# A streaming-encoder block in split fp32: start addresses of weights and moving tiles, and seven other offsets in one product

## The chip, the core and the metric

The kernel runs on one NeuronCore of a Trainium2 chip. The metric is device time in microseconds of one execution, lower is better. One launch computes the whole block; weights and input lie in the chip's DRAM, and the working set is tiled into the core's on-chip memory, SBUF, which has 128 partitions. An address below is a byte offset within a partition.

## The reference, cut to what matters

One layer, 512 tokens, 1024 channels, all in float32:

```python
x = x + 0.5 * swiglu(rms_norm(x, ffn1_norm), ffn1_w1, ffn1_w3, ffn1_w2)      # D_FF = 2816
p = rms_norm(x, mix_norm) @ w_in
y_a = rwkv7_mixer(...) @ rwkv_proj       # delta rule, 8 heads x 64
y_b = fox_mixer(...) @ fox_proj          # forgetting attention, 8 heads x 64
x = x + (gate_a * y_a + gate_b * y_b) @ w_out
x = x + 0.5 * swiglu(rms_norm(x, ffn2_norm), ffn2_w1, ffn2_w3, ffn2_w2)
out = rms_norm(x, final_norm)

def swiglu(h, w1, w3, w2):
    return (silu(h @ w1) * (h @ w3)) @ w2
```

## The kernel before

Channels stand on the partitions, the 512 tokens along the free axis. The input is transposed into eight tiles xT of 128 x 512. A matmul takes a weight tile of 128 x 128 as its stationary operand and a tile of 128 x 512 as its moving operand, and accumulates into one bank of PSUM.

**Split products.** For the accuracy of float32 every operand is split in two float32r tiles, hi (a rounded copy) and lo (what is left). `mm3` (L124) then issues three matmuls for one product: hi by hi, hi weights by lo moving, lo weights by hi moving (L125 to L127). Nearly all of TensorE's time is in these three lines.

**Weights.** `load_raw` issues one DMA on the SyncE queue into one of 3 `raw` buffers. `split_w` (L111) makes `whi` with a cast on ScalarE (L117) and `wlo` with a subtract on VectorE (L118), each in one of 2 buffers. So a weight piece can be cast only when TensorE has finished the piece two before it, and loaded only when the piece three before it has been split.

**Stages, in the order of time.** The first FFN: for each of 22 column tiles the products `pa` and `pb` over 8 normalized tiles xh/xl, then on VectorE and ScalarE silu and product into hh and hl, 22 tiles each. Its last product `pd` (L340 to L346) runs over 8 output tiles m and, for each, over 22 k-tiles; the 22 weight tiles come in the pieces of `cuts` (L338): 8, 8 and 6 k-tiles. Then the mixer: projections of w_in (`pl`, `pk`, `pgt`, `pq`, `pv`), the RWKV recurrence and the attention with many short matmuls, the two output projections `ppj` (moving yh/yl, then ya) and w_out's `pw` (moving mh/ml). Then the second FFN with the same function `ffn`; its `pd` has seven output tiles of this kind. After each, VectorE adds the result to the residual tile xS, TensorE transposes that (`ot`), and VectorE writes it with the final gain into O. The eighth output tile has weights of its own (`ownh`, `ownl`) and runs in two halves of 256 tokens.

**What sets the order.** Tiles come from pools that allocate SBUF one after the other, on the left and the right side, so that a tile's address follows from the sizes of those before it. The instruction order of each engine is made by a scheduler in the program's build, from a timeline of its own; engines synchronize through semaphores.

Of the kernel before, what the change touches and what calls it, by code (L numbers as in the profile page):

```python
# [9 lines left out]
F32 = mybir.dt.float32  # L10
F32R = mybir.dt.float32r
BF16 = mybir.dt.bfloat16
AF = mybir.ActivationFunctionType
ALU = mybir.AluOpType
# [4 lines left out]
P = 128  # L19
T = 512  # L20
D = 1024
KD = D // P
# [3 lines left out]
NP = DA // P  # L26
C = 32
NC = T // C
NB = T // P
# [6 lines left out]
PAR_W0, PAR_A0, PAR_KK, PAR_KA, PAR_RK, PAR_LG, PAR_LB = 38, 42, 46, 50, 54, 58, 62  # L36
PAR_Q, PAR_K, PAR_F = 66, 67, 68
PAR_N = 69

COL_W = 3 * DA  # L40
COL_G = COL_W + 64
# [9 lines left out]
def kernel(  # L51
# [7 lines left out]
    dve, act, pool, pe = nc.vector, nc.scalar, nc.gpsimd, nc.tensor  # L59

    cp = ctx.enter_context(tc.tile_pool(name="cp", bufs=1))
    xp = ctx.enter_context(tc.tile_pool(name="xp", bufs=1))
    wp = ctx.enter_context(tc.tile_pool(name="wp", bufs=2))
    tp = ctx.enter_context(tc.tile_pool(name="tp", bufs=4))
# [5 lines left out]
    def bank(name, pool_=None):  # L70
        pool_ = pool_ or pm
        return pool_.tile([P, T], F32, tag="b", name=name)

    def tmp(name, shape=(P, T), dt=F32, tag="t", **kw):
        return tp.tile(list(shape), dt, tag=tag, name=name, **kw)
# [3 lines left out]
    make_identity(nc, ident)  # L79
    identb = cp.tile([P, P], BF16, name="identb")  # L80
    dve.tensor_copy(identb[:], ident[:])
    ones = cp.tile([P, P], F32, name="ones")
    dve.memset(ones[:], 1.0)
    onesr = cp.tile([P, P], F32R, name="onesr")
    dve.tensor_copy(onesr[:], ones[:])
    bones = tmp("bones", (P, P))
    dve.memset(bones[:], 0.0)
    dve.memset(bones[0:64, 0:64], 1.0)
# [15 lines left out]
    def load_raw(aps, kt, n):  # L104
        raw = wp.tile([P, kt, n], F32, tag="raw", name="raw", bufs=3)
        for c0, src in aps:
            nc.sync.dma_start(raw[:, :, c0:c0 + src.shape[1]],
                              src.rearrange("(k p) c -> p k c", p=P))
        return raw

    def split_w(raw, kt, n, eng=None, own=None):  # L111
        if own is None:
            hi = wp.tile([P, kt, n], F32R, tag="whi", name="whi", bufs=2)
            lo = wp.tile([P, kt, n], F32R, tag="wlo", name="wlo", bufs=2)
        else:
            hi, lo = [xp.tile([P, kt, n], F32R, tag=f"x{i}{own}", name=f"own{i}{own}") for i in "hl"]
        act.copy(hi[:], raw[:])  # L117
        (eng or dve).tensor_tensor(lo[:], raw[:], hi[:].bitcast(F32), op=ALU.subtract)  # L118
        return hi, lo

    def load_w(aps, kt, n, eng=None, own=None):
        return split_w(load_raw(aps, kt, n), kt, n, eng, own)

    def mm3(ps, whi, wlo, xhi, xlo, first, last):  # L124
        pe.matmul(ps, whi, xhi, start=first, stop=False)  # L125
# [78 lines left out]

    par = cp.tile([P, PAR_N], F32, name="par")

# [5 lines left out]
    nc.scalar.dma_start(g1[:], ffn1_norm[0].rearrange("(a b) -> a b", b=P))  # L212
    warm = bank("warm", pf)
    for _ in range(8):
        pe.matmul(warm[:, 0:P], ones[:], ones[:], start=True, stop=True)
    gtp = bank("gtp", pr)
    pe.transpose(gtp[:, 0:8], g1[:], ident[0:8, 0:8])
    dve.tensor_copy(par[:, 0:8], gtp[:, 0:8])
# [28 lines left out]
    tc.keep_in_program_order(pin)  # L247
    rows = rtp.tile([PAR_N, P], F32, name="rows")
    loraw = rtp.tile([P, DA], F32, name="loraw")
# [45 lines left out]
    def place_params():  # L295
        ptp = bank("ptp")
        pe.transpose(ptp[:, 0:PAR_N], rows[:], ident[0:PAR_N, 0:PAR_N])
        dve.tensor_copy(par[:, 8:PAR_N], ptp[:, 8:PAR_N])
        dve.tensor_scalar(par[:, PAR_Q:PAR_Q + 1], par[:, PAR_Q:PAR_Q + 1], 0.125, None, op0=ALU.mult)
# [8 lines left out]
    def ffn(nrm, w1, w3, w2, nxt, during=(), first=None, final=None):  # L308
        with tc.tile_pool(name="hp", bufs=1) as hp:
            hh, hl = [], []  # L310
            for j in range(KF):
                c0 = j * P
                if j == 0 and first:
                    pa, pb = [f[0] for f in first]
                else:
                    pa = bank("pa")
                    pb = bank("pb", pr)
                    for ps, w in ((pa, w1), (pb, w3)):
                        nrm.cols(ps[:], *load_w([(0, w[0][:, c0:c0 + P])], KD, P), P)
                if j == 0:  # L320
                    nrm.finish()
                if j in during:
                    with tc.issue_after(pin.ins):
                        during[j]()
                a = tmp("fa")
                dve.tensor_tensor(a[:], pa[:], nrm.rstd[:], op=ALU.mult)  # L326
                sa = tmp("fs")
                act.activation(sa[:], a[:], AF.Silu)
                b = tmp("fb")
                dve.tensor_tensor(b[:], pb[:], nrm.rstd[:], op=ALU.mult)  # L330
                h = tmp("fh")
                dve.tensor_tensor(h[:], b[:], sa[:], op=ALU.mult)
                hi = hp.tile([P, T], F32R, name=f"hh{j}")
                lo = hp.tile([P, T], F32R, name=f"hl{j}")
                split(hi[:], lo[:], h[:], "dve")
                hh.append(hi)
                hl.append(lo)
            cuts = ((0, 8), (8, 8), (16, 6))  # L338

            for m in range(KD - (final is not None)):  # L340
                ps = bank("pd")
                for k0, kn in cuts:
                    wh, wl = load_w([(0, w2[0][k0 * P:(k0 + kn) * P, m * P:(m + 1) * P])], kn, P)
                    for k in range(k0, k0 + kn):
                        mm3(ps[:], wh[:, k - k0, :], wl[:, k - k0, :], hh[k][:], hl[k][:], k == 0, k == KF - 1)
                dve.scalar_tensor_tensor(xT[m][:], ps[:], 0.5, xT[m][:], op0=ALU.mult, op1=ALU.add)  # L346
                nxt(m)
            if final is not None:
                m = KD - 1
                quarters = [(k0, min(4, KF - k0)) for k0 in range(0, KF, 4)]  # L350
                ws = [load_w([(0, w2[0][k0 * P:(k0 + kn) * P, m * P:(m + 1) * P])], kn, P, own=i)
                      for i, (k0, kn) in enumerate(quarters)]
                for h in range(2):
                    ps = bank("pd")
                    cols = slice(h * T // 2, (h + 1) * T // 2)
                    for (k0, kn), (wh, wl) in zip(quarters, ws):
                        for k in range(k0, k0 + kn):
                            mm3(ps[:, 0:T // 2], wh[:, k - k0, :], wl[:, k - k0, :], hh[k][:, cols], hl[k][:, cols],
                                k == 0, k == KF - 1)
                    dve.scalar_tensor_tensor(xT[m][:, cols], ps[:, 0:T // 2], 0.5, xT[m][:, cols],  # L360
                                             op0=ALU.mult, op1=ALU.add)
                    final(h)
# [16 lines left out]
    with ExitStack() as mx:  # L379
        rp = mx.enter_context(tc.tile_pool(name="rp", bufs=1))  # L380
# [13 lines left out]

        nka = rp.tile([P, NP], F32, name="nka")
        dve.tensor_scalar(nka[:], par[:, PAR_KA:PAR_KA + NP], -1.0, None, op0=ALU.mult)
        tiny = rp.tile([P, 2], F32, name="tiny")
        dve.memset(tiny[:, 0:1], 1e-24)
        dve.memset(tiny[:, 1:2], -1e-24)
        omu = rp.tile([P, PAR_W0 - PAR_MU], F32, name="omu")  # L400
        dve.tensor_scalar(omu[:], par[:, PAR_MU:PAR_W0], -1.0, 1.0, op0=ALU.mult, op1=ALU.add)

        def shifted(o, src, rows, mu):
            act.activation(o[0:rows, :], src[0:rows, :], AF.Copy, scale=omu[0:rows, mu - PAR_MU:mu - PAR_MU + 1])
# [49 lines left out]
        xctx.close()  # L454
        fctx = ExitStack()
        vtp = fctx.enter_context(tc.tile_pool(name="vtp", bufs=1, side="right"))
        pctx = ExitStack()
        t2 = pctx.enter_context(tc.tile_pool(name="t2", bufs=1, side="right"))
        cmask = t2.tile([P, T], F32, name="cmask")
        pool.memset(cmask[:], 1.0)  # L460
        pool.memset(cmask[:].rearrange("p (c t) -> p c t", t=C)[:, :, 0:1], 0.0)

        PC = rp.tile([P, NP, NC], F32, name="PC")
        Ld = dp.tile([P, C, C], F32, name="Ld")
        Td = dp.tile([P, C, C], F32, name="Td")
        V4 = rp.tile([P, NP, T], F32, name="V4", tag="V4")
# [142 lines left out]
        for t in range(C - 1):  # L609
            n, m = t + 1, C - 1 - t  # L610
# [7 lines left out]
        for i in range(2):  # L618
            for q in range(2):
                o = i * 64 + q * C  # L620
# [57 lines left out]
        vt = []  # L678
# [6 lines left out]
                    mm3(vps[b][:], mix.hi[kk][:, bs], mix.lo[kk][:, bs], wh[:, k, :], wl[:, k, :],  # L685
                        kk == 0, kk == KD - 1)
        for b in range(NB):
            o = vtp.tile([P, T], F32, name=f"vt{b}", tag=f"vt{b}")
            act.activation(o[:], vps[b][:], AF.Copy, scale=rc[:, b:b + 1])
            vt.append(o)  # L690
        plain_gate(NP)
# [10 lines left out]
        for q in range(2):  # L702
            pool.memset(Rs[0][half(q), :, q, :], 0.0)
            for i in range(4):
                o = (1 - q) * 64
# [21 lines left out]
        for c in range(NC):  # L727
# [3 lines left out]
            for p, q in heads():  # L731
                o = (p // 2) * 64 + q * C
# [41 lines left out]
        for q in range(2):  # L774
            o = (1 - q) * 64
            pool.memset(f32(klc[q][:]), 0.0)
            dve.tensor_copy(klc[q][o:o + 8, :], fz[FR, :])
        for q in range(2):
            o = (1 - q) * 64
# [8 lines left out]
        for p in range(NP):  # L788
# [5 lines left out]
            for q in range(2):  # L794
# [6 lines left out]
                dve.tensor_tensor(klc[q][h_, :], kp[h_, :], f32(kb[q][h_, :]), op=ALU.subtract)  # L801
                act.copy(qb[q][h_, :], qp[h_, :])
                dve.tensor_copy(qb[q][g_, :], sel[g_, h:h + 1].broadcast_to([64, T]))
            mx_ = [tp.tile([P, 2 * NB], F32, tag=f"mx{q}", name=f"mx{q}", bufs=2) for q in range(2)]
            for i, bl in enumerate(((0, 1), (2,), (3,))):
                at = {b: sum(c + 1 for c in bl[:j]) * P for j, b in enumerate(bl)}
                w = sum(b + 1 for b in bl) * P
                lps, trs = [], []
                for q in range(2):
                    lp = pf.tile([P, T], F32, tag="b", name="lp")  # L810
                    lps.append(lp)
                    for b in bl:
                        n, bs = (b + 1) * P, slice(b * P, (b + 1) * P)
# [4 lines left out]
                for q in range(2):  # L818
                    pt, mx = pts[:, q], mx_[q]
                    for b in bl:  # L820
                        n, mb = (b + 1) * P, mx[:, b:b + 1]
# [17 lines left out]
                for j, b in enumerate(bl):  # L839
                    for k in range(b + 1):  # L840
                        o = at[b] + k * P
# [61 lines left out]
        for p in range(NP):  # L903
            o = vtp.tile([P, T], F32R, name=f"yh{p}", tag=f"vt{p}")
# [39 lines left out]
        for m in range(KD):  # L944
            wh, wl = load_w([(0, w_out[0][:, m * P:(m + 1) * P])], KD, P)
# [78 lines left out]
```

## Time and profile before

| | |
|---|---|
| timed runs, median (lowest to highest) | 1213.7 us (1209.55 to 1213.95), 3 runs |
| span of the profiled execution | 1210.2 us (its time beyond the span is not listed) |
| TensorE busy | 1184.5 us of the span, 6334 matmuls |
| VectorE, ScalarE, GpSimd busy | 665.2, 458.1, 100.5 us |
| mean granted TensorE clock | 0.992 |
| DMA | 122.54 MB, mean 101 GB/s |

How to read it: the span is from the first to the last instruction of one execution. A matmul's record reaches from its start to its modelled end and overlaps the next one's, so the time that a matmul costs is read from one start to the next, not from its duration. A row of the timeline gives start and duration in us, engine, line, operation, the tile written and those read; a row of the windows view gives length, then each engine's busy time with its count, the granted clock, the DMA share and GB/s. A row of the view of one tile gives minimum, median and maximum duration in ns, and the first and last start in us.

### The profile page before, as it was taken

What the parts mean: (1) busy time and instruction counts of PE and PEld (TensorE: products, weight loads), DVE (VectorE), ACT (ScalarE), POOL (GpSimd) and SP (SyncE); (2) the same over time, 40 slices, a digit from 0 to 9 for tenths busy, and PEclk for the clock granted to TensorE, in tenths of its full rate; (3) what the DMA queues carried; (4) which work ended last, traced back from release to release, by engine and by line L of the source; (5) the groups of instructions that cost most, each with busy time, mean ns of one, the idle gap of its engine ahead of it and who ended that gap; (6) DMA issues with size and microseconds to landing.
All of it is one profiled execution on the core that took longest, in us unless ns stands there. A gap on an engine that the chain in (4) does not pass through costs nothing.

```text
span 1210.2 us, 15874 instructions
## 1 busy us (share of the span) xinstructions
PE 1184.5 (98%) x6334; PEld 955.1 (79%) x6334; DVE 665.2 (55%) x993; ACT 458.1 (38%) x739; POOL 100.5 (8%) x144
## 2 busy tenths in 40 slices
PE   8999999999999999999999999999999999999997
PEld 6788888888887788887667777678888888888887
DVE  7454555443443688776766666865554445443232
ACT  5222222222222854445867655523322222222221
POOL 4100000001111111321000011111000000000110
PEclk9999999999999999999999999999999999999999
DMA  6233233333334234345113235532333333323331
GB/s 186 73 95 105 87 105 88 104 95 108 107 111 106 76 104 124 109 135 131 36 36 102 63 97 163 178 106 87 103 102 92 100 104 88 104 80 96 96 96 70
DMA packets 208152, 122.54 MB, mean 101 GB/s; under 512 B 9902, under 2 KB 200430, under 8 KB 208078
## 3 DMA queue, kind: packets, MB, share of 16 engines
q1 hardware_dynamic: 202078, 108.67, 31.1%
q0 software_dynamic: 3760, 12.06, 3.2%
q8 instruction: 50, 0.82, 0.3%
q10 hardware_dynamic: 2240, 0.79, 0.3%
q14 instruction: 24, 0.20, 0.1%
HBM read 110.82 MB, written 10.68 MB: 100 GB/s over the span
## 4 chain that ended last, share of the span: by engine, by line
PE 93%; DVE 3%; ACT 1%; issue 0%; DMA 0%; DVEq 0%; POOL 0%; POOLq 0%
PE pd L127 7%; PE pd L125 7%; PE pd L126 7%; PE pa L125 7%; PE pa L126 7%; PE pa L127 6%; PE pb L127 6%; PE pb L126 6%; PE pb L125 6%; PE pgt L125 3%; PE pgt L127 2%; PE pgt L126 2%; PE pk L125 2%; PE pk L127 2%; PE pk L126 2%; PE pw L127 1%
## 5 line engine op out<-in xcount | busy, mean ns | idle before, releaser
L117 ACT CAST whi<-raw 128x1024 fp32r<-128x1024 f32 (+3 forms) x199 | 198.2, 998 | 631.2 <-PE pa L126 180.7
L118 DVE TENSOR_TENSOR wlo<-raw,whi 128x1024 fp32r<-128x1024 f32 (+2 forms) x198 | 229.5, 1159 | 142.3 <-ACT whi L117 142.2
L125 PE MATMUL pa<-xh,whi 128*128 128x512 f32 x344 | 134.7, 392 | 2.6 <-DVE fa L326 2.6
L127 PE MATMUL pb<-xh,wlo 128*128 128x512 f32 x344 | 134.5, 391 | 0.9 <-DVE wlo L118 0.9
L126 PE MATMUL pa<-xl,whi 128*128 128x512 f32 x344 | 134.6, 391 | 0.0
L125 PE MATMUL pb<-xh,whi 128*128 128x512 f32 x344 | 134.5, 391 | 0.0
L126 PE MATMUL pb<-xl,whi 128*128 128x512 f32 x344 | 134.5, 391 | 0.0
L127 PE MATMUL pa<-xh,wlo 128*128 128x512 f32 x344 | 134.4, 391 | 0.0
L127 PE MATMUL pd<-hh,wlo 128*128 128x512 f32 x330 | 130.8, 396 | 0.0
L125 PE MATMUL pd<-hh,whi 128*128 128x512 f32 x330 | 130.3, 395 | 0.0
L126 PE MATMUL pd<-hl,whi 128*128 128x512 f32 x330 | 130.3, 395 | 0.0
L330 DVE TENSOR_TENSOR fb<-pb,rstd 128x512 f32<-128x512 f32 x43 | 29.7, 691 | 137.5 <-PE pb L127 137.5
L125 PEld LDWEIGHTS pa<-xh,whi 128*128 128x128 f32 x344 | 64.9, 189 | 16.7 <-DVE fa L326 3.1
L127 PEld LDWEIGHTS pb<-xh,wlo 128*128 128x128 f32 x344 | 65.0, 189 | 14.8 <-DVE wlo L118 1.3
L127 PEld LDWEIGHTS pa<-xh,wlo 128*128 128x128 f32 x344 | 65.0, 189 | 13.6
L126 PEld LDWEIGHTS pa<-xl,whi 128*128 128x128 f32 x344 | 65.0, 189 | 13.5
L126 PEld LDWEIGHTS pb<-xl,whi 128*128 128x128 f32 x344 | 65.0, 189 | 13.5
L125 PEld LDWEIGHTS pb<-xh,whi 128*128 128x128 f32 x344 | 64.9, 189 | 13.5
L126 PEld LDWEIGHTS pd<-hl,whi 128*128 128x128 f32 x330 | 62.0, 188 | 14.9
L125 PEld LDWEIGHTS pd<-hh,whi 128*128 128x128 f32 x330 | 62.0, 188 | 14.6
L127 PEld LDWEIGHTS pd<-hh,wlo 128*128 128x128 f32 x330 | 62.0, 188 | 14.6
L326 DVE TENSOR_TENSOR fa<-pa,rstd 128x512 f32<-128x512 f32 x43 | 29.7, 692 | 73.6 <-PE pa L127 73.6
(395 smaller groups left out, 1968.0 us busy)
## 6 DMA issues: line engine op xcount, KB each, us to landing
raw<-in_ffn_w_dram SPq DMA_DIRECT2D x118, 512.0 KB
raw<-in_w_in_dram SPq DMA_DIRECT2D x40, 512.0 KB
raw<-in_ffn_w_dram SPq DMA_DIRECT2D x15, 384.0 KB
raw<-in_w_out_dram SPq DMA_DIRECT2D x8, 512.0 KB
gsave<-gs SPq DMA_DIRECT2D x9, 256.0 KB
xin<-in_x_dram SPq DMA_DIRECT2D x4, 512.0 KB
xsave<-xT POOLq DMA_DIRECT2D x8, 256.0 KB, 2.3
G<-gsave POOLq DMA_DIRECT2D x8, 256.0 KB, 3.8
```

Source lines behind the costliest of these rows:

```text
L117: act.copy(hi[:], raw[:])
L118: (eng or dve).tensor_tensor(lo[:], raw[:], hi[:].bitcast(F32), op=ALU.subtract)
L125: pe.matmul(ps, whi, xhi, start=first, stop=False)
L126: pe.matmul(ps, whi, xlo, start=False, stop=False)
L127: return pe.matmul(ps, wlo, xhi, start=False, stop=last)
L326: dve.tensor_tensor(a[:], pa[:], nrm.rstd[:], op=ALU.mult)
L330: dve.tensor_tensor(b[:], pb[:], nrm.rstd[:], op=ALU.mult)
```

## The change

No product, no dtype and no buffer count changes. Two things do.

**Start addresses.** Three small constants are moved or padded: `ones` becomes a view of `onesr` with its first copy in a temporary buffer, `tiny` and `mx_` are padded to 32 columns, `PC` is allocated earlier, the `vt` tiles are allocated when their pool is opened, with 48 columns behind them. The tiles after them shift. In the program as built, byte addresses modulo 512 are:

| operands of a product | before | after |
|---|---|---|
| all weights (whi, wlo, ownh, ownl) of full 128-column tiles | 288 | 288 (but see below) |
| xh, xl (moving in `pa`, `pb`, `pk`, `pgt`, `pq`) | 288 | 288 |
| hh, hl (moving in `pd`) | 416 | 288 |
| ya, mh, ml (moving in `ppj`, `pw`) | 320 | 288 |
| yh, yl (moving in the first `ppj`) | 480 | 288 |
| kb, klc, qa (attention) | 480 | 288 |

A full weight tile is 512 bytes wide and a moving tile 2048, so a whole row of k-tiles keeps its place modulo 512. Only weights that are cut narrower (`pl`, 72 and 96 columns) wander.

**The second FFN's last product.** There, for the output tiles m = 0 to 6, `split_w` puts hi and lo at `PLACES[m]` columns into a buffer of full size. The weights thus start 4 * PLACES[m] bytes further than the moving tile, modulo 512: 256, 128, 64, 32, 16, 448 and 192. To leave room for it, `cuts` has there four pieces of 6, 6, 6 and 4 k-tiles in place of 8, 8 and 6. The first FFN keeps its three pieces and its place 0.

```diff
+PAD = 32
+PLACES = (64, 32, 16, 8, 4, 112, 48)
...
-    ones = cp.tile([P, P], F32, name="ones")
-    dve.memset(ones[:], 1.0)
+    ones_ = tmp("ones", (P, P))
+    dve.memset(ones_[:], 1.0)
     onesr = cp.tile([P, P], F32R, name="onesr")
-    dve.tensor_copy(onesr[:], ones[:])
+    dve.tensor_copy(onesr[:], ones_[:])
+    ones = onesr[:].bitcast(F32)
...
-    def split_w(raw, kt, n, eng=None, own=None):
-        if own is None:
+    def split_w(raw, kt, n, eng=None, own=None, place=0):
+        if place:
+            hi, lo = [wp.tile([P, KD * P], F32R, tag=f"w{i}", name=f"w{i}", bufs=2) for i in ("hi", "lo")]
+            hi, lo = [t[:, place:place + kt * n].rearrange("p (k c) -> p k c", c=n) for t in (hi, lo)]
+        elif own is None:
...
-            cuts = ((0, 8), (8, 8), (16, 6))
+            cuts = ((0, 8), (8, 8), (16, 6)) if final is None else ((0, 6), (6, 6), (12, 6), (18, 4))
...
-                    wh, wl = load_w([(0, w2[0][k0 * P:(k0 + kn) * P, m * P:(m + 1) * P])], kn, P)
+                    wh, wl = load_w([(0, w2[0][k0 * P:(k0 + kn) * P, m * P:(m + 1) * P])], kn, P,
+                                    place=0 if final is None else PLACES[m])
...
-        tiny = rp.tile([P, 2], F32, name="tiny")
+        tiny = rp.tile([P, PAD], F32, name="tiny")
...
+        PC = rp.tile([P, NP, NC], F32, name="PC")
...
+        vts = [vtp.tile([P, T], F32, name=f"vt{b}", tag=f"vt{b}") for b in range(NB)]
+        vtp.tile([P, 48], F32, name="vtpad", tag="vtpad")
...
-            mx_ = [tp.tile([P, 2 * NB], F32, tag=f"mx{q}", name=f"mx{q}", bufs=2) for q in range(2)]
+            mx_ = [tp.tile([P, PAD], F32, tag=f"mx{q}", name=f"mx{q}", bufs=2) for q in range(2)]
```

Up to the second FFN's last product each engine's instructions stand in the same order as before. From there on the weights' pieces move. First VectorE at the turn of one output tile, before: `wlo` is a piece's subtract, xS the residual add of the tile that ends, O the write after its transposes.

```order
L118 TENSOR_TENSOR wlo<-raw,whi 128x768
L118 TENSOR_TENSOR wlo<-raw,whi 128x1024
L346 SCALAR_TENSOR_TENSOR xS_6470<-pd,xS_6470 128x512
L118 TENSOR_TENSOR wlo<-raw,whi 128x1024
L967 TENSOR_TENSOR O<-ot,fg 128x4x128
```

And the same place now:

```order
L125 TENSOR_TENSOR wlo<-raw,whi 128x512
L125 TENSOR_TENSOR wlo<-raw,whi 128x768
L354 SCALAR_TENSOR_TENSOR xS_6471<-pd,xS_6471 128x512
L125 TENSOR_TENSOR wlo<-raw,whi 128x768 x2
L978 TENSOR_TENSOR O<-ot,fg 128x4x128
```

In both the next tile's first piece (row 2) stands ahead of the residual add; now the third piece's subtract is also ahead of O.

Then TensorE at the transposes `ot` of the tile that ended, before, within the new tile's eighth k-tile, the last of its first piece:

```order
L125 MATMUL pd<-hh_7604,whi 128x512
L126 MATMUL pd<-hl_7605,whi 128x512
L965 MATMUL ot<-ident,xS_6472 128x128 x4
L127 MATMUL pd<-hh_7604,wlo 128x512
L125 MATMUL pd<-hh_7678,whi 128x512
```

And now, at the seventh k-tile, which is the first of the second piece:

```order
L132 MATMUL pd<-hh_7531,whi 128x512
L133 MATMUL pd<-hl_7532,whi 128x512
L976 MATMUL ot<-ident,xS_6473 128x128 x4
L134 MATMUL pd<-hh_7531,wlo 128x512
L132 MATMUL pd<-hh_7605,whi 128x512
```

The transposes come one k-tile earlier. The matmuls of each tile keep their sequence; in the seventh tile the first matmuls of the eighth tile are mixed in somewhat earlier.

More of the change, by code (lines that the diff above doesn't have):

```diff
@@ L116, in split_w, with load_w @@
             hi, lo = [xp.tile([P, kt, n], F32R, tag=f"x{i}{own}", name=f"own{i}{own}") for i in "hl"]
-        act.copy(hi[:], raw[:])
-        (eng or dve).tensor_tensor(lo[:], raw[:], hi[:].bitcast(F32), op=ALU.subtract)
+        hi, lo = [t if place else t[:] for t in (hi, lo)]
+        act.copy(hi, raw[:])
+        (eng or dve).tensor_tensor(lo, raw[:], hi.bitcast(F32), op=ALU.subtract)
         return hi, lo
-    def load_w(aps, kt, n, eng=None, own=None):
-        return split_w(load_raw(aps, kt, n), kt, n, eng, own)
+    def load_w(aps, kt, n, eng=None, own=None, place=0):
+        return split_w(load_raw(aps, kt, n), kt, n, eng, own, place)
     def mm3(ps, whi, wlo, xhi, xlo, first, last):
@@ L214 @@
     for _ in range(8):
-        pe.matmul(warm[:, 0:P], ones[:], ones[:], start=True, stop=True)
+        pe.matmul(warm[:, 0:P], ones_[:], ones_[:], start=True, stop=True)
     gtp = bank("gtp", pr)
@@ L461 @@
         pool.memset(cmask[:].rearrange("p (c t) -> p c t", t=C)[:, :, 0:1], 0.0)
-        PC = rp.tile([P, NP, NC], F32, name="PC")
         Ld = dp.tile([P, C, C], F32, name="Ld")
@@ L687 @@
         for b in range(NB):
-            o = vtp.tile([P, T], F32, name=f"vt{b}", tag=f"vt{b}")
+            o = vts[b]
             act.activation(o[:], vps[b][:], AF.Copy, scale=rc[:, b:b + 1])
```

## The prediction

> **What bounds the kernel now.** I read the page's busy times and chain first, then the groups of matmuls, then the timeline at the places where the matmul's operands change.
>
> ```profile
> PE 1184.5 (98%) x6334; PEld 955.1 (79%) x6334; DVE 665.2 (55%) x993; ACT 458.1 (38%) x739; POOL 100.5 (8%) x144
> PE 93%; DVE 3%; ACT 1%; issue 0%; DMA 0%; DVEq 0%; POOL 0%; POOLq 0%
> ```
>
> TensorE is busy for 98% of the span and holds 93% of the chain that ended last. Nothing else is near it, so what counts is how long one matmul holds TensorE, and whether anything makes it wait.
>
> ```profile
> 100.00:200.00 100.00, 100.00 (x443) 82.80 (x442) 51.30 (x68) 24.29 (x27) 0.00 (x0) 1.00 0.33 95
> ```
>
> This window lies inside the first FFN's first half, where only `pa` and `pb` run. A window counts a matmul that began up to 0.39 us before it, about 1.7 here, so 100 us / 441.3 = **226.6 ns** from one start to the next. Its operands, xh/xl and whi/wlo, all start at byte 288 modulo 512.
>
> ```profile
> 261.72 0.39 PE L126 MATMUL pb<-xl,whi 128*128 128x512 f32 x1
> 261.95 0.39 PE L127 MATMUL pb<-xh,wlo 128*128 128x512 f32 x1
> 262.17 0.40 PE L125 MATMUL pd<-hh,whi 128*128 128x512 f32 x1
> 262.41 0.39 PE L126 MATMUL pd<-hl,whi 128*128 128x512 f32 x1
> 262.63 0.40 PE L127 MATMUL pd<-hh,wlo 128*128 128x512 f32 x1
> 262.87 0.39 PE L125 MATMUL pd<-hh,whi 128*128 128x512 f32 x1
> 263.10 0.40 PE L126 MATMUL pd<-hl,whi 128*128 128x512 f32 x1
> 263.34 0.39 PE L127 MATMUL pd<-hh,wlo 128*128 128x512 f32 x1
> ...
> 262.00:386.00 124.00, 123.36 (x528) 99.06 (x528) 5.27 (x8) 1.00 0.37 107
> ```
>
> The timeline shows the edge between `pb` and `pd`: the steps are 0.23, 0.22, then 0.24, 0.22, 0.24, 0.23, 0.24. Nothing waits, the shape and the weights' place are unchanged; only the moving tile is another, hh at byte 416. The last row is all of the first FFN's last product: (123.36 - 0.16 of the last one's tail) / 528 = **233.3 ns**. It keeps that step for 123 us at a granted clock of 1.00.
>
> Is it the address? The view of one tile gives minimum, median and maximum of a matmul's recorded duration, which is its step plus about 162 ns of pipeline.
>
> ```profile
> L126 PE MATMUL pa<-xl,whi x344: 389/389/632, 37.6 to 1068.8; 128*128 128x512 f32 x172
> ...
> L126 PE MATMUL pd<-hl,whi x176: 387/395/398, 262.4 to 384.9; 128*128 128x512 f32 x176
> ...
> L126 PE MATMUL pw<-ml,whi x64: 392/396/398, 788.6 to 834.3; 128*128 128x512 f32 x64
> ...
> L126 PE MATMUL ppj<-yl,whi x32: 388/394/398, 733.4 to 760.9; 128*128 128x512 f32 x32
> ...
> L126 PE MATMUL pl<-xl,whi x16: 387/394/400, 385.6 to 396.5; 128*72 128x512 f32 x8, 128*96 128x512 f32 x8
> ```
>
> `pa` has 389 as its minimum and its median. Three products with moving tiles at 416, 320 and 480 have 394 to 396. `pl` decides more: it moves the same xl as `pa`, but its weights are 72 and 96 columns wide, so their starts wander over many bytes modulo 512, and it too has 394. So it is neither the tile nor its data, but how the two operands lie to each other. Equal is the only relation in which the trace shows a constant step.
>
> **The change, part by part.** Every matmul and its order stay up to the second FFN's last product; the steps change.
>
> *First FFN's last product.* hh and hl come to byte 288, the relation of `pa`. 528 x (233.3 - 226.6) = **-3.5 us**, all on the path, since TensorE has no gap there.
>
> *The projections `ppj` and w_out's `pw`.* 192 + 192 matmuls come to 288 against 288. 395 - 389 = 6 ns, 384 x 6 = -2.3 us. Not all of it counts. Part of `ppj` stands under a chain of ScalarE and VectorE:
>
> ```profile
> 763.40 0.70 ACT Tall L893
> 764.12 0.64 ACT Tall L894
> 764.79 0.70 DVE V L895
> ...
> 770.70 0.52 ACT whi L117
> 771.26 0.51 PE ppj L125
> ```
>
> From 763.4 to 771.3 faster matmuls only wait longer; some 26 run there (0.2 us). And after an interruption the equal relation has to settle:
>
> ```profile
> 397.62 0.39 PE L126 MATMUL pk<-xl,whi 128*128 128x512 f32 x1
> ...
> 398.77 0.39 PE L125 MATMUL pk<-xh,whi 128*128 128x512 f32 x1
> ...
> 400.81 0.39 PE L125 MATMUL pk<-xh,whi 128*128 128x512 f32 x1
> ```
>
> In `pk`, equal too, the first 5 steps after a transpose take 1.15 us (230 each), the next 9 take 2.04 (226.7). That is 17 ns for each interruption, here some ten: 0.1 to 0.2 us. I take **-2.0 us**.
>
> *The second FFN's last product, tiles 0 to 6.* 7 x 66 = 462 matmuls go from one unequal relation (416 against 288) to seven others: the weights lie 256, 128, 64, 32, 16, 448 and 192 bytes further than the moving tile. The trace has these distances only mixed, in `pl`.
>
> ```profile
> 1136.02 0.39 PE L125 MATMUL pd<-hh,whi 128*128 128x512 f32 x1
> ...
> 1142.31 0.40 PE L125 MATMUL pd<-hh,whi 128*128 128x512 f32 x1
> ...
> 1161.14 0.39 PE L127 MATMUL pd<-hh,wlo 128*128 128x512 f32 x1
> ...
> 1167.64 0.39 PE L125 MATMUL pd<-hh,whi 128*128 128x512 f32 x1
> ```
>
> Now 27 steps take 6.29 us (233.0) in one tile and 28 steps 6.50 us (232.1) in another, 232.6 on average. The ends: all seven as the equal pair, 462 x -6 = -2.8 us; all seven at the longest common record, 398 - 162 = 236, +1.6 us. The nearest rows are the unequal ones, at 232 to 234, but 16 and 32 bytes are close to equal, and I expect one or two of the seven to lock: **-0.8 us**.
>
> *The last tile's halves.* 132 matmuls of 256 columns, also brought to equal.
>
> ```profile
> 1189.89 0.28 PE L125 MATMUL pd<-hh,ownh 128*128 128x256 f32 x1
> ...
> 1192.97 0.28 PE L127 MATMUL pd<-hh,ownl 128*128 128x256 f32 x1
> ...
> 629.26 0.63 PE L126 MATMUL pgt<-xl,whi 128*128 128x512 f32 x1
> ...
> 630.97 0.63 PE L127 MATMUL pgt<-xh,wlo 128*128 128x512 f32 x1
> ...
> 628.60:632.00 3.40, 3.40 (x13) 2.17 (x10) 2.85 (x8) 1.81 (x5) 0.00 (x0) 0.50 0.00 0
> ```
>
> 26 steps take 3.08 us, 118.5 each. No equal pair of this width is in the trace. At a granted clock of 0.50 four steps of 512 columns take 1.71 us, 427 each, so the columns alone need 213.5 at full clock and 107 for half of them; the equal pair adds 13. If it adds 13 here, the step is 120 (+0.2 us); if half of that, 113.5 (-0.7 us). I take 0, between the nearest row and these.
>
> *Four pieces.* Per tile one more load, cast and subtract, each shorter. The longer row of TensorE's work stays the same, so the cost is only a wait. The critical one is the next tile's first piece, whose buffers come free at the end of piece 3 and which must be ready after the short piece 4: 12 x 0.2326 = 2.8 us.
>
> ```profile
> 1127.19 0.84 ACT L117 CAST whi<-raw 128x768 fp32r<-128x768 f32 x1 [4.03 <-PE pd L126]
> ...
> 1128.20 0.95 DVE L118 TENSOR_TENSOR wlo<-raw,whi 128x768 fp32r<-128x768 f32 x1
> ...
> 1137.61 0.69 DVE L346 SCALAR_TENSOR_TENSOR xS<-pd,xS 128x512 f32<-128x512 f32 x1 [2.13 <-PE pd L127]
> ...
> 1171.94 0.37 SPq L107 DMA_DIRECT2D raw<-in_ffn_w_dram  x1
> ...
> 1174.13 0.62 ACT L117 CAST ownh<-raw 128x512 fp32r<-128x512 f32 x1 [2.97 <-DMA raw<-in_ffn_w_dram]
> ```
>
> Cast 0.84 and subtract 0.95 make 1.8 us, against 2.8, and wlo is wanted two matmuls later still. The residual add xS (0.69) stands behind this subtract in the new order, so nothing is ahead of it; behind it wait only the add, which the transposes need 4 us later. A load of 256 KB takes 2.2 us from issue to the cast that it releases, so one of 384 KB takes some 3.3 by bytes, against three pieces (over 11 us) of prefetch. The cover is about 1 us per tile; cost **0**. If it is gone, each us late is paid seven times.
>
> The rest (padded constants, `ones` as a view of `onesr`, early places for vt and PC) changes addresses alone, by -0.2 to +0.2 us in the short matmuls of the mixer; 0.
>
> Sum: -3.5 - 2.0 - 0.8 + 0 + 0 = **-6.3 us**. Against the profiled execution's span of 1210.2 us that gives 1203.9. The page gives no other time of that execution; the three timed runs lie between 0.7 us under its span and 3.8 above, with the median at 1213.7, so I forecast 1213.7 - 6.3 = **1207.4 us**. Stretches at half clock like the one above cost 3.4 x (1 - 226.6/427) = 1.6 us each; one more or fewer moves a run by that, in either direction.
>
> **The rivals.** *Addresses do nothing*: `pd` is slow for another reason and stays at 233. Then nothing is gained: 1213.7. `pl` speaks against it. The Trainium skill's page "TensorE: Matmul & The Clock Gate", section "Step-by-step: what each phase is for", is for it: TensorE has two independent read ports, so that "Loading the next tile's weights doesn't steal SBUF read bandwidth from the running matmul." By that rule the sum is 0; the 389 and 395 above, with the same weight loads beside them, do not agree. 8%.
>
> *Only the moving tile's own start counts, not the relation*: all pairs with 288 lock, the seven tiles too, and the third term is -2.8 in place of -0.8: 1205.4. `pl` speaks against this as well. 10%.
>
> *The odd places are worse than now*: the seven tiles at 236, third term +1.6: 1209.8. 8%.
>
> *Slower*: the next tile's first piece comes late after the short fourth one. Cover is 1 us; each us beyond it is paid at seven tiles. The 5.5 us gained without the third term are eaten at 0.8 us late (in all 1.8 us more than the rows say); at 2 us late the kernel is at 1213.7 - 5.5 + 14 = 1222. Rows speak against it: all operations are known. 2%.
>
> **How the numbers follow.** The forecast gets 72%. Its own range is 1205 to 1210 (third term, last halves, one half-clock stretch). The range of 8 in 10 is **1203.5 to 1211.5**: it takes in the second and third rivals and leaves out the first and the last. What a measurement can tell is about 0.5%, 6.1 us; my -6.3 stands on that edge. Faster by more: somewhat over half of the 72% (0.40) and all of the 10%: 0.50. Slower: 0.02. Within: 0.48.
>
> **What would show it.** In the first FFN's `pd` a median record of 389 (step 226.6, 119.7 us for the product); `pw` and `ppj` at 389; the seven tiles each with a median of their own, most from 392 to 398; no gap ahead of a tile's first matmul; the last halves between 113 and 120 ns per step. A `pd` that still alternates at 288 would fell the first term, and with it the forecast.

## The result, and the profile after

| | before | after |
|---|---|---|
| timed runs, median (lowest to highest) | 1212.22 us (1209.55 to 1213.95), 4 runs | **1205.53 us** (1204.27 to 1207.04), 4 runs |
| ratio, 95% interval | | **0.9946** (0.9928 to 0.9965) |
| span of the profiled execution | 1210.2 us | 1204.6 us |

The ratio stands for 6.5 us, its interval for 4.2 to 8.7. TensorE is still the bound. From the page of the kernel after, the busy times and the chain that ended last:

```profile
PE 1176.9 (98%) x6334; PEld 955.2 (79%) x6334; DVE 663.9 (55%) x1000; ACT 460.2 (38%) x746; POOL 98.7 (8%) x144
...
PE 92%; DVE 3%; ACT 1%; issue 0%; DVEq 0%
```

The same 6334 matmuls are busy for 7.6 us less, and seven casts and seven subtracts have come (746 against 739, 1000 against 993). From the timeline of after, the same edge in the first FFN, from `pb` to its last product `pd`; and from the view of the tile `pd`, that product alone (minimum, median and maximum of a record in ns, first and last start):

```profile
262.48 0.39 PE L134 MATMUL pb<-xh,wlo 128*128 128x512 f32 x1
262.70 0.39 PE L132 MATMUL pd<-hh,whi 128*128 128x512 f32 x1
262.93 0.39 PE L133 MATMUL pd<-hl,whi 128*128 128x512 f32 x1
263.16 0.39 PE L134 MATMUL pd<-hh,wlo 128*128 128x512 f32 x1
263.38 0.39 PE L132 MATMUL pd<-hh,whi 128*128 128x512 f32 x1
```

```profile
L133 PE MATMUL pd<-hl,whi x176: 389/389/389, 262.9 to 381.9; 128*128 128x512 f32 x176
```

The edge can no longer be seen in the steps: 0.22, 0.23, 0.23, 0.22, with hh now at 288. All 176 records of one line last 389 ns, where before they lasted 387 to 398. The projections have it too (views of the tiles `pl`, `ppj` and `pw` of after; `pl`, whose weights still wander, has not):

```profile
L133 PE MATMUL pl<-xl,whi x16: 389/396/398, 382.6 to 393.5; 128*72 128x512 f32 x8, 128*96 128x512 f32 x8
```

```profile
L133 PE MATMUL ppj<-yl,whi x32: 387/389/397, 730.2 to 757.3; 128*128 128x512 f32 x32
```

```profile
L133 PE MATMUL pw<-ml,whi x64: 389/389/397, 784.6 to 829.1; 128*128 128x512 f32 x64
```

**The second FFN's last product, tile by tile.** Below is the windows view of after, with TensorE alone: from:to, length, busy time with its count, clock, DMA share, GB/s. Each window lies in one output tile where no transposes interrupt, is a whole number of steps long, and starts 0.05 us after a matmul has started. Two earlier records reach into it, so the steps are the count less 2, and length over steps is the time of one matmul.

```profile
1069.92:1084.20 14.28, 14.28 (x65) 1.00 0.29 83
1089.75:1099.55 9.80, 9.80 (x44) 1.00 0.28 80
1105.59:1115.39 9.80, 9.80 (x44) 1.00 0.27 80
1121.43:1131.22 9.79, 9.79 (x44) 1.00 0.27 80
1137.26:1147.06 9.80, 9.80 (x44) 1.00 0.28 81
1153.02:1162.64 9.62, 9.62 (x44) 1.00 0.28 82
1173.55:1179.14 5.59, 5.59 (x26) 1.00 0.42 120
```

In this order the weights lie 256, 128, 64, 32, 16, 448 and 192 bytes further than the moving tile. The steps are **226.7**, 233.3, 233.3, 233.1, 233.3, 229.0 and 232.9 ns. The one that locked (kept the short step) is the most distant, 256; 16 and 32 did not lock. The last window lies behind the place where the eighth tile's first matmuls are mixed into the seventh. Ahead of that place the same tile, at the same 192 bytes, runs faster:

```profile
1163.33:1167.45 4.12, 4.12 (x20) 1.00 0.43 127
```

18 steps, 228.9 ns each. So an unequal pair does not have one step of its own: after an interruption it can settle in another one.

**Where the 5.6 us between the two profiled executions come from.** The marks are starts in both traces, at rows shown here or in the prediction; `pb` of the second FFN ends so (views of that tile, after, then before):

```profile
L134 PE MATMUL pb<-xh,wlo x344: 389/389/500, 29.6 to 1069.2; 128*128 128x512 f32 x172
```

```profile
L127 PE MATMUL pb<-xh,wlo x344: 389/389/628, 27.5 to 1074.4; 128*128 128x512 f32 x172
```

| stretch, from mark to mark | before, us | after, us | change |
|---|---|---|---|
| start to first `pd` | 262.2 | 262.7 | +0.5 |
| first FFN's `pd`, to `pl`'s second matmul | 123.4 | 119.9 | -3.5 |
| mixer, to `ppj`'s second matmul | 347.8 | 347.6 | -0.2 |
| `ppj` and `pw`, to its last k-tile | 100.9 | 98.9 | -2.0 |
| second FFN, `pa` and `pb`, to the last of `pb` | 240.1 | 240.1 | 0.0 |
| second FFN's `pd`, to the end | 135.8 | 135.4 | -0.4 |

The first row of the table fits the granted clock. Up to the first `pd` the execution of before had two half-clock windows (stretches of 3.4 us at a granted clock of 0.50), that of after three, and that of the kernel with hh/hl alone moved (below) four; they reach `pd` at 262.2, 262.7 and 263.2 us. Two of after's three lie at its very start, where TensorE is also idle part of the time (busy 5.08 of 7.50 us), which would explain why the third costs less there than the 1.6 us of a busy stretch. The windows view of after:

```profile
7.00:14.50 7.50, 5.08 (x18) 0.54 1.06 305
```

### The profile page after: what moved, and what is told of

Its sections match the earlier page's. It is cut to its first block, busy times and chain, and to the rows that moved or that the text cites. A ratio compares the mean times of both kernels' runs of the same rounds, so it can differ in the third digit from the quotient of the medians.

```text
span 1204.6 us, 15914 instructions
## 1 busy us (share of the span) xinstructions
PE 1176.9 (98%) x6334; PEld 955.2 (79%) x6334; DVE 663.9 (55%) x1000; ACT 460.2 (38%) x746; POOL 98.7 (8%) x144
## 4 chain that ended last, share of the span: by engine, by line
PE 92%; DVE 3%; ACT 1%; issue 0%; DVEq 0%
PE pd L132 7%; PE pd L134 7%; PE pd L133 7%; PE pa L132 7%; PE pa L134 7%; PE pa L133 7%; PE pb L134 6%; PE pb L133 6%; PE pb L132 6%; PE pgt L132 3%; PE pgt L134 2%; PE pgt L133 2%; PE pk L132 2%; PE pk L133 2%; PE pk L134 2%; PE pw L134 1%
## 5 line engine op out<-in xcount | busy, mean ns | idle before, releaser
L125 DVE TENSOR_TENSOR wlo<-raw,whi 128x1024 fp32r<-128x1024 f32 (+2 forms) x205 | 230.7, 1126 | 161.1 <-ACT whi L124 161.0
```

The lines of the kernel that those rows point to most:

```text
L125: (eng or dve).tensor_tensor(lo, raw[:], hi.bitcast(F32), op=ALU.subtract)
```

## The experiments

**What one half-clock window does to a comparison.** One of 3.4 us costs 1.6 us (the prediction) and lowers a run's mean granted clock by 3.4 x 0.5 / 1207 = 0.0014, so 0.001 of clock is some 1.1 us by this estimate. A straight line through clock and time of the nineteen timed runs of before that stand beside these experiments gives more, 2.0 us. Each timed run has its mean clock with it; I use that where an effect is as small.

### All places equal, with three pieces and with four

Theories: the relation of weights and moving tile sets the step (all tiles at 226.7 where they are equal); or the tiles of the second FFN are slow for a reason of their own. With three pieces:

```diff
-PLACES = (64, 32, 16, 8, 4, 112, 48)
+PLACES = (0,) * 7
...
-            cuts = ((0, 8), (8, 8), (16, 6)) if final is None else ((0, 6), (6, 6), (12, 6), (18, 4))
+            cuts = ((0, 8), (8, 8), (16, 6))
```

> The changed kernel with place 0 and three pieces (8, 8, 6) in the second FFN too, so that every long product has its weights and its moving tile at byte 288 modulo 512. Relation theory: all 15 output tiles of pd step at 226.7 ns (median record 389); against the changed kernel the six tiles that are still at 229 to 233 give 66 x (6.4 + 6.6 + 6.6 + 6.5 + 2.7 + 4.3 ns) = 2.2 us, so some 1203.3 us, ratio to before about 0.9926. Rival (nothing more to gain, because something else ends the tail): within 0.5 us of the changed kernel's 1205.5.

Measured: 1203.82 us, ratio 0.9929 (0.9914 to 0.9944). The same with the four pieces kept (the first hunk alone):

> The changed kernel with place 0 in all seven tiles, but still four pieces (6, 6, 6, 4). Against e1_all_equal it shows the price of the pieces alone. Theory that the cover holds: no gap ahead of any first matmul of a tile, within 0.3 us of e1_all_equal. Rival (each turn of a tile costs): a gap of x us at seven tiles, 7x us slower.

Measured: 1203.34 us, ratio 0.9927 (0.9912 to 0.9941). Windows as above, of the second and third tile with three pieces:

```profile
1091.87:1100.75 8.88, 8.88 (x41) 1.00 0.15 45
1107.33:1116.19 8.86, 8.86 (x41) 1.00 0.15 45
```

Steps of 227.7 and 227.2. So the seven tiles too can have the short step, and the odd places give up about 2 us of what equal addresses bring. Between three and four pieces the timed runs show no difference, and in the two traces the stretch from the last of `pb` to the end takes 133.4 and 133.5 us. Neither kernel can be told from the kernel after by the intervals of the times (0.9928 to 0.9965 overlaps both); it is the steps that tell them apart.

### The moving tiles hh/hl alone, and the mixer alone

Each takes the kernel before and moves one group of tiles to 288.

```diff
         with tc.tile_pool(name="hp", bufs=1) as hp:
+            hp.tile([P, 96], F32, name="hpad", tag="hpad")
             hh, hl = [], []
```

> The kernel before with one unused tile of 96 columns ahead of hh and hl, which brings these from byte 416 to 288 and moves nothing else; three pieces, ppj and pw as before. Relation theory: pd at 226.7 in both FFNs, 528 x 6.66 + 456 x 6.1 ns = 3.5 + 2.8 us gained, the last halves 120 in place of 118.6 ns lose 0.1 to 0.2: 6.1 us, ratio 0.995; ppj and pw stay at 233. Rival (the gain of the change is not the address of hh, but lies in the other constants and orders): pd stays near 233 and the time at 1212.

Measured: 1207.78 us, ratio 0.9964 (0.9952 to 0.9977). For the mixer alone (its moving tiles and `ones`, with 120 columns of padding in place of the padded constants):

```diff
+    ones = onesr[:].bitcast(F32)
...
+        rp.tile([P, 120], F32, name="rpad", tag="rpad")
...
+        vts = [vtp.tile([P, T], F32, name=f"vt{b}", tag=f"vt{b}") for b in range(NB)]
+        vtp.tile([P, 48], F32, name="vtpad", tag="vtpad")
```

> The kernel before with the new early places of the vt tiles, the 48 columns behind them, 120 unused columns ahead of the mixer's tiles, and ones as a view of onesr (for room), so that ya, mh, ml, yh, yl come to byte 288 while hh stays at 416. Relation theory: ppj and pw at 226.7, their excess falls from 2.4 to 0.2 or 0.3 us; of that 1.9 to 2.1 us show in the time (some matmuls stand under a chain of ScalarE and VectorE), ratio about 0.9984; pd stays at 233. Rival (waits take it all back): time unchanged, with longer gaps ahead of ppj and pw.

Measured: 1209.77 us, ratio 0.9982 (0.9972 to 0.9993). From the views of the tiles `pd` (first FFN) and `pw`, first of the kernel with hh/hl moved:

```profile
L126 PE MATMUL pd<-hl,whi x176: 389/389/389, 263.4 to 382.4; 128*128 128x512 f32 x176
...
L126 PE MATMUL pw<-ml,whi x64: 392/396/398, 785.1 to 830.9; 128*128 128x512 f32 x64
```

and of the kernel with the mixer moved:

```profile
L127 PE MATMUL pd<-hl,whi x176: 387/395/398, 262.2 to 384.7; 128*128 128x512 f32 x176
...
L127 PE MATMUL pw<-ml,whi x64: 387/389/397, 789.4 to 834.0; 128*128 128x512 f32 x64
```

Each part does its own work and leaves the other's alone. The first part's time fell short: the means of the times are 1207.68 and 1211.85, so 4.2 us were gained where 6.1 were expected. In its trace the first FFN's `pd` takes 119.9 us in place of 123.4, and the stretch from the last of `pb` to the end 133.5 in place of 135.8: 5.8 us, nearly what was expected. The rest goes with the clock: its seven runs had a mean granted clock of 0.9904, the nineteen of before 0.9919, and 0.0015 of clock is 1.7 us by the lower of the two figures. That the lower clock is chance and not the padding isn't proved by seven runs, but the kernels with all places equal have the same hh/hl place and mean clocks of 0.9917 and 0.9934.

### Weights and moving tiles both at another byte

Rival: only the moving tile's start at 288 counts. Here hh/hl stay at 416 as before, and `pd`'s weights go there in both FFNs (place 32), in four pieces.

```diff
-            cuts = ((0, 8), (8, 8), (16, 6))
+            cuts = ((0, 6), (6, 6), (12, 6), (18, 4))
...
-                    wh, wl = load_w([(0, w2[0][k0 * P:(k0 + kn) * P, m * P:(m + 1) * P])], kn, P)
+                    wh, wl = load_w([(0, w2[0][k0 * P:(k0 + kn) * P, m * P:(m + 1) * P])], kn, P, place=32)
```

> The kernel before, with hh and hl where they were (byte 416), and the weights of both pd products brought to byte 416 by place 32, in four pieces. Relation theory: equal at another byte is as good, all 15 tiles at 226.7 (median 389), some 6 us less than before; the eighth tile's own weights stay at 288 and its halves at 118.6 ns. Rival (what counts is that the moving tile, or all, start at 288): pd stays at 232 to 234.

Measured: 1203.87 us in one run, before 1210.49 beside it. The view of `pd` in the first FFN, then a window in the second:

```profile
L130 PE MATMUL pd<-hl,whi x176: 389/389/389, 263.2 to 382.2; 128*128 128x512 f32 x176
```

```profile
1089.07:1098.61 9.54, 9.54 (x44) 1.00 0.27 82
```

389 and 227.1: byte 416 does as well as 288, if both have it. The rival has fallen.

### Which distances lock

A rival to "only equal locks" (256 counts as equal here) was a tolerance of a few bytes: then the nearest places, 4 and 8 bytes off, would keep 226.7 ns. The expected time is the same in both cases, so the steps decide. The places here give +4, +8, +12, -4, -8, -16 and -32 bytes:

```diff
-PLACES = (64, 32, 16, 8, 4, 112, 48)
+PLACES = (1, 2, 3, 127, 126, 124, 120)
```

> The changed kernel with the seven tiles' weights 4, 8, 12 bytes after and 4, 8, 16, 32 bytes before the moving tile's start modulo 512, four pieces. [...] If only exact equality (or 256) holds: all seven at 229 to 234. The time is 1204 to 1206 in both.

Measured (1205.2 us in one run), in windows as above, the first six tiles:

```profile
1068.63:1083.27 14.64, 14.64 (x65) 1.00 0.28 81
1088.78:1098.47 9.69, 9.69 (x44) 1.00 0.27 81
1104.44:1114.25 9.81, 9.81 (x44) 1.00 0.27 80
1120.29:1130.10 9.81, 9.81 (x44) 1.00 0.28 80
1136.12:1145.92 9.80, 9.80 (x44) 1.00 0.27 81
1151.86:1161.45 9.59, 9.59 (x44) 1.00 0.28 82
```

232.4, 230.7, 233.6, 233.6, 233.3 and 228.3; the seventh tile, 32 bytes before, has 233.3 (24 steps in 5.60 us). 4 bytes are about as bad as 128, and 4 is one float32: there is no tolerance. Then the distances of after with 256 added, and others; if the relation counts modulo 256, 320 must behave as 64, 288 as 32, 272 as 16 and 260 as 4:

```diff
-PLACES = (64, 32, 16, 8, 4, 112, 48)
+PLACES = (48, 112, 80, 72, 68, 65, 24)
```

> The changed kernel with distances 192, 448, 320, 288, 272, 260 and 96 bytes. If the relation counts modulo 256: 192 and 448 come out alike, 320 like 64 (233.3, records of 231 and 235/236 in turn), 288 like 32 (235, 232), 272 like 16 (233, 232, 235), 260 like 4. If 256 is a case of its own in a period of 512: 320, 288 and 272 differ from 64, 32 and 16 by more than 1 ns on average.

Measured (1207.13 us in one run), for 192, 448, 320, 288, 272 and 260 bytes:

```profile
1070.49:1084.91 14.42, 14.42 (x65) 1.00 0.27 82
1090.39:1100.02 9.63, 9.63 (x44) 1.00 0.29 82
1106.05:1115.85 9.80, 9.80 (x44) 1.00 0.27 80
1121.89:1131.69 9.80, 9.80 (x44) 1.00 0.27 80
1137.72:1147.52 9.80, 9.80 (x44) 1.00 0.27 81
1153.54:1163.30 9.76, 9.76 (x44) 1.00 0.28 81
```

228.9, 229.3, 233.3, 233.3, 233.3 and 232.4; the seventh tile, at 96, has 233.8 (24 steps in 5.61 us). The last four of the six equal their partners without the 256 to 0.2 ns (233.3, 233.1, 233.3, 232.4), and 192 and 448 are alike. The relation counts **modulo 256**; that is why 256 locked in after.

### Hi and lo apart

Is it the matmul's own weights, or those being loaded beside it? Call A the matmul hh by whi, B hl by whi, C hh by wlo, in their order. Beside B the lo weights are loaded, beside C and A the hi weights. First, hi and lo at places of their own in the second FFN (a pair is hi, lo, in columns; "16 bytes" in the expectation are 16 columns, 64 bytes):

```diff
+PLACES = ((0, 32), (32, 0), (0, 16), (16, 0), (0, 64), (64, 0), (0, 0))
...
-            hi, lo = [t[:, place:place + kt * n].rearrange("p (k c) -> p k c", c=n) for t in (hi, lo)]
+            hi, lo = [t[:, at:at + kt * n].rearrange("p (k c) -> p k c", c=n) for t, at in zip((hi, lo), place)]
```

> The changed kernel with hi and lo weights at different places: in tile 0 lo, in tile 1 hi 128 bytes off, in 2 and 3 lo and hi 16 bytes, in 4 and 5 lo and hi 256 bytes, tile 6 both equal. Three matmuls make one product: hi by hi, hi by lo moving, lo by hi. If a matmul is disturbed by the load of the next weights that runs beside it, lo off disturbs the second of the three (its neighbour loads lo) and hi off the first and the third. If its own weights disturb it, lo off disturbs the third and hi off the first two. 256 disturbs none. Which of the three carries the step above 227 tells it; since a step also shifts the next one's start, the sums may spread over all three, and then it stays open.

Measured (1206.44 us in one run): the tiles with lo or hi at 256 have 227.6 to 227.9 a step, as modulo 256 wants. With lo apart by 128 the mean is 231.1, with hi 233.6, but the transposes throw most tiles out of step, so A, B and C can't be read there. The first FFN has no transposes. So there, in four pieces, with the pairs (0, 32), (32, 0), (0, 16), (16, 0), (0, 48), (48, 0), (32, 32), (0, 4), and with the second FFN all equal in three:

> In the first FFN's last product, where nothing interrupts the row, hi and lo weights lie at different distances from the moving tiles; everything else is equal. Tiles 0, 2, 4: lo alone at 128, 64, 192 bytes; tiles 1, 3, 5: hi alone at the same; tile 6: both at 128; tile 7: lo at 16. A, B, C as above. Theory 1, the weights loaded beside the running matmul count (the load of C's lo runs beside B): with lo apart B is longer and A and C are at 226.7; with hi apart (loads beside C and A) B is at 226.7. Theory 2, the matmul's own weights count: with lo apart only C is longer, with hi apart A and B. If both count: with lo apart B and C, A at 226.7; with hi apart all three. Tile 6 about 233 as in the kernel before; tile 4, at 192, about 229 to 231 where it is longer.

And all weights equal, in three pieces, with hl alone apart, which B alone moves:

```diff
-PLACES = (64, 32, 16, 8, 4, 112, 48)
+PLACES = (0,) * 7
...
+            his = [hp.tile([P, T], F32R, name=f"hh{j}") for j in range(KF)]
+            apart = 32 if final is None else 48
+            hp.tile([P, apart], F32, name="hpad", tag="hpad")
+            los = [hp.tile([P, T], F32R, name=f"hl{j}") for j in range(KF)]
```

> All weights and moving tiles equal, but hl alone lies elsewhere: 128 bytes from its weights (modulo 256) in the first FFN, 64 in the second. Call A the matmul hh by whi, B hl by whi, C hh by wlo, which follow one another. B is the only one whose moving tile is apart, both from its own weights (whi) and from those loaded beside it (wlo). If the relation decides each matmul by itself: A and C at 226.7 ns, B alone longer, by 5 to 8 ns; the product costs 176 x 6.5 = 1.1 us more than all equal in the first FFN. If an unequal matmul also throws the one after it out of step: C is longer too, 2.3 us in all. If the moving tile's own place counts for nothing: all at 226.7.

Measured: 1205.38 us with hl apart and 1201.88 with the weights apart, one run each beside 1211.85 of before (the second had a mean clock of 0.996, few half-clock windows, so its time is not a gain). The view of `pd` in the first FFN with hl apart:

```profile
L132 PE MATMUL pd<-hh,whi x176: 389/389/389, 263.3 to 383.5; 128*128 128x512 f32 x176
L133 PE MATMUL pd<-hl,whi x176: 395/395/395, 263.5 to 383.7; 128*128 128x512 f32 x176
L134 PE MATMUL pd<-hh,wlo x176: 388/388/390, 263.8 to 383.9; 128*128 128x512 f32 x176
```

With the weights apart, its tiles 0 (lo at 128 bytes), 1 (hi at 128) and 7 (lo at 16):

```profile
L133 PE MATMUL pd<-hl,whi x22: 395/397/397, 261.5 to 276.0; 128*128 128x512 f32 x22
L134 PE MATMUL pd<-hh,wlo x21: 396/397/398, 261.7 to 275.6; 128*128 128x512 f32 x21
L132 PE MATMUL pd<-hh,whi x21: 388/389/390, 261.9 to 275.8; 128*128 128x512 f32 x21
...
L133 PE MATMUL pd<-hl,whi x22: 395/396/398, 276.7 to 291.5; 128*128 128x512 f32 x22
L134 PE MATMUL pd<-hh,wlo x22: 394/398/398, 277.0 to 291.7; 128*128 128x512 f32 x22
L132 PE MATMUL pd<-hh,whi x21: 392/394/402, 277.2 to 291.2; 128*128 128x512 f32 x21
...
L133 PE MATMUL pd<-hl,whi x21: 388/390/390, 368.3 to 381.9; 128*128 128x512 f32 x21
L134 PE MATMUL pd<-hh,wlo x21: 389/390/390, 368.6 to 382.2; 128*128 128x512 f32 x21
L132 PE MATMUL pd<-hh,whi x20: 389/390/390, 368.8 to 381.7; 128*128 128x512 f32 x20
```

With hl apart B alone is long, so here a long matmul does not lengthen the next. With lo apart by 128 both B (lo loaded beside it) and C (lo its own) are long and A is not; with hi apart all three are. At 128 bytes, then, it looks as if both relations count. The other tiles of this run fit that only in part. With lo apart by 64 and 192 bytes B and C are again long (medians of B 392 and 395, of C 398 and 392) and A is not (390 and 389); but with hi apart by 64 A is not long (389, 398, 394 for A, B, C), and by 192 C is not (393, 391, 389). And lo at 16 costs nothing, though hi and lo both at 16 cost the full step in after, in a tile that transposes interrupt. No simple rule of the three covers all of this, and the mechanism stays open.

## Why the prediction was right, and where its steps were not

The median of 1205.53 us lies in the range, 1.9 below the forecast. Of these 1.9, 1.5 are the base: 1213.7 was the median of three runs of before, four have 1212.22 and the nineteen later ones 1211.62. The change itself was forecast as -6.3 and came as -6.7 against the four and -6.1 against the nineteen. Faster by more than 0.5% had 0.50 and within it 0.48; 0.54% with its interval (0.35 to 0.72) does not decide between them. By its steps:

**First FFN's `pd`, -3.5**: measured -3.5, at a median record of 389 as said. Shown by the kernel that moves hh/hl alone: the same 119.9 us.

**`ppj` and `pw`, -2.0**: measured -2.0; both at 389. Shown by the kernel that moves the mixer alone.

**The seven tiles, -0.8**: the size came out near by luck, the reason was wrong. The step that failed is "16 and 32 bytes are close to equal, and I expect one or two of the seven to lock". Nearness does nothing: 4 bytes off is at 232.4. What locked was 256 bytes, since the relation counts modulo 256, and 448 came part of the way, to 229.0. Behind that step lies "modulo 512", which I took from the table of addresses. The trace of before could show a pair 256 apart only mixed, in `pl`. The measured sum is -0.6. The first tile's mean went from 233.2 to 226.8, 66 x 6.4 = -0.4 us; the sixth gave -0.2, the seventh -0.1 (232.7 to 231.0 over the whole tile), and the four others together lost 0.1.

**Last halves, 0 (ends +0.2 and -0.7)**: the dearer end came. From the timeline of after:

```profile
1180.73 0.28 PE L132 MATMUL pd<-hh,ownh 128*128 128x256 f32 x1
...
1183.13 0.28 PE L134 MATMUL pd<-hh,ownl 128*128 128x256 f32 x1
```

20 steps in 2.40 us, 120.0 each against 118.5 before: at both widths the equal pair adds 13 ns to its columns (226.7 - 213.5 and 120.0 - 107), so a fixed amount and not a share. Over 132 matmuls that is +0.1 to +0.2 us.

**Four pieces, 0 with a cover of 1 us**: right; with all places equal four pieces took 0.1 us more than three from the last of `pb` to the end. The turn of a tile in after, on ScalarE and VectorE (start, duration, and in brackets the idle time and what ended it), and the next tile's first matmul:

```profile
1097.37 0.83 ACT L124 CAST whi<-raw 128x768 fp32r<-128x768 f32 x1 [3.58 <-PE pd L133]
...
1098.23 0.96 DVE L125 TENSOR_TENSOR wlo<-raw,whi 128x768 fp32r<-128x768 f32 x1 [3.72 <-ACT whi L124]
...
1100.20 0.40 PE L132 MATMUL pd<-hh,whi 128*128 128x512 f32 x1
```

The piece's buffer comes free at 1097.37, it is split at 1099.19, and the first matmul starts at 1100.20 with no wait: the cover is 1.0 us. At no other turn of these seven tiles does TensorE wait either. So the slower rival never came near its point of 0.8 us late.

**The rivals.** "Addresses do nothing" is out: one padding tile moves 528 matmuls from 233.3 to 226.7. By the rule of the Trainium skill's page "TensorE: Matmul & The Clock Gate", section "Step-by-step: what each phase is for", TensorE reads moving data and weights through two separate ports, so that loading the next weights takes no read bandwidth from the running matmul. Here, with the same loads beside them, the step is 226.7 or 233.3 ns by how the two addresses lie to each other, and the measurement decides. "Only the moving tile's own start counts" fell in after itself, where the moving tiles of all seven start at 288 and one locks, and with both at 416. "Odd places are worse" was half right: four of seven tiles run at 233.1 to 233.3, just above their mean of before, but none at 236.

**The range.** One half-clock window more at the start took back 0.5 us in the profiled run, inside what was allowed for.

## What to carry to other kernels

Where TensorE runs without gaps in float32r, with a weight load beside every matmul and moving tiles of 512 columns, place weights and moving tiles at the same address modulo 256 bytes; here it is worth 6.7 ns of 233 per matmul, about 8 us of 1212 where every product has it, and costs a padding tile. Other types were not run. Read the step from one start to the next in windows a whole number of matmuls long, by operand pair: a mean over a line mixes pairs that lock with pairs that don't. When an effect is under 1%, put each run's mean granted clock beside its time.

## What was not expected of the hardware

- The relation counts modulo 256 bytes: 0 and 256 give 226.7 ns, and of the thirteen other distances modulo 256 that were tried with hi and lo together (4 to 252) none does; they give 228.3 to 233.8.
- It is a step, not a slope: 4 bytes apart already costs 5.7 ns. The smallest excess is at 240 bytes (228.3) and at 192 (228.9 to 229.3), not next to 0; and 192 has a second step, 232.9, behind an interruption in the same tile.
- For moving tiles of 256 columns the equal pair is the slower one, 120.0 against 118.5 ns.
- An address that is apart by 128 bytes in the moving tile alone costs only that tile's matmul; one that is apart by 128 in the lo weights alone costs the matmul beside their load as well as their own.
